# A streaming-encoder layer: an empty tile on the right stack, earlier queries, another bank for the gate scale

## The chip, the cores and the metric

The kernel runs on one core of one Trainium2 chip. The metric is the device time of one execution in microseconds (us), lower is better. Three timed runs of the kernel before gave 1702.1, 1703.69 and 1704.55 us; the median is 1703.69 us. The trace comes from one further, profiled execution.

## The reference, cut to what matters

One layer of a hybrid encoder on 1024 prompt tokens and 64 sample tokens, width 1024. Everything is f32.

```python
z = rmsnorm(x) @ w_in            # split: qa ka va (heads A) | qi ki wi (indexer) | qb kb vb (heads B) | ga gb (gates)
# A: isc[t,s] = sum_h wi[t,h] * relu(qi[t,h] . ki[s]); keep the top 256 keys (48 for samples); attention over them
# B: attention over the own 64-token chunk and the 8 chunks before, with a bias by relative distance
m = sigmoid(ga) * (oa @ w_o_a) + sigmoid(gb) * (ob @ w_o_b)
x = x + m @ w_out
y = x + square(relu(rmsnorm(x) @ w_up)) @ w_down
```

## The kernel before, in words

Tokens are worked on in nine blocks: 0 to 7 are the prompt (128 tokens each), block 8 holds the 64 samples. Each f32 product is made of three matmuls on high and low halves (`three`, L152), or two where one side is stacked (`two`, L161). The normalised input lies in SBUF turned, as `xnT` with high and low parts. A scheduler that works from an estimate of every instruction's time fixes the order of each engine's queue when the program is built: instructions that stand earlier in the program go first, and later ones fill in where an engine would be idle. `tc.issue_after(ins)` holds what its block issues on the engine of `ins` behind `ins`.

The stages that matter here, in order:

- **Indexer** (L392 to L472). `x` arrives in five pieces of 256 tokens (the last has 64). `cut_piece` splits a piece into `xnT`: eight copies on ACT (L267), eight subtractions on DVE (L268). `stage_keys(i)` multiplies block i with the 264 key columns, `stage_norms(i)` normalises and rotates the key (its last step is a GpSimd copy, L333), `stage_queries(i)` multiplies with the 320 query columns into a PSUM bank with the tag `acc` (two of them). `stage_scores(i)` first turns the key on TensorE into a bank `pt` (two of them; `index_keys`, L230: turn, ACT copy `kih`, DVE subtraction `kil`), then turns the queries, then makes the scores in banks `s` (four of them). Before, the order is: keys 0 to 5, scores 0 to 2, queries 4 and 5, piece 3, scores 3, keys 6 and 7, piece 4, scores 4, keys 8, queries 6 to 8.
- **Head projections** (`project_heads`, L512) and, beside them on DVE and ACT, the search for the top-k threshold (`choose`, L605). The results go through banks `acc` (2) and `wide` (4, which take the place of `s`, L598). `rows_to_dram` (L482) turns them in a bank `pt`.
- **Early gates** (L734 to L755): the first four rows of gate products, each three chunks of 24 matmuls in banks `wide` and `acc`. Each sum is multiplied on DVE with `spread` (L686), a tile that holds every token's scale on all partitions. `spread` is made by three sets of transposes (L731), in banks `pt`, each with an ACT copy (L733). The weights of these gates lie in the pool `pj`. `mask_out` (L661) then reads the scores in the pool `works` and writes the masks.
- **Attention** (L774 to L902): heads 0 to 7 of kind B, then 8 of kind A. `load_head` (L689) brings a head's `qT`, `kh`, `kl`, values and, for B, the bias (`turned`). Head 0 goes into a pool on the left and is loaded early; head 1 goes into `at`, on the right. `probs` (L781) records the first matmul of every score chunk in `marks`, 13 in a head. The eight middle rows of gates (L914) are fillers: 192 groups of three matmuls, of which group number i is held behind mark number i times 208/188 (`next_mark`, L908). Their weights come through `columns_of` (L762), which has its tiles in the pool `ring`: three `raw`, five `hi`, five `lo`.

SBUF pools are two stacks, `left` and `right`. On the right lie, from the outside: `fw` (8224 bytes a partition by its tiles: rope, five gains, two fold tiles, four rope temporaries), `works` (17824: the per-token scales and the scores), and on top of these first `ixw`, later `pj`, and `tk`. At L757 `tk`, `pj`, `works` and `fw` are closed; then `ring` is opened in their place (13 tiles of 2048 bytes: 26624) and `at` on top of it. `fw` and `works` end at byte 26048, where `pj` begins.

Of the kernel before, what the change touches and what calls it, by code (L numbers as in the profile page):

```python
# [10 lines left out]
F32 = mybir.dt.float32  # L11
# [7 lines left out]
P = 128  # L19
D = 1024  # L20
KB = D // P
TP = 1024
TS = 64
T = TP + TS
NT = TP // P
H = 8
HD = 64
# [17 lines left out]
def kernel(  # L45
# [8 lines left out]
    nc = tc.nc  # L54
# [26 lines left out]
    def bank(tag, n=512):  # L81
        pool, bufs = banks[tag]
        return pool.tile([P, n], F32, tag=tag, name=tag, bufs=bufs)
# [5 lines left out]
    def open_pool(name, side="left", **reuse):  # L89
        st = ExitStack()  # L90
        p = st.enter_context(tc.tile_pool(name=name, bufs=1, side=side, **reuse))
        pools[name] = st
        return p

    def close_pool(name):
        pools.pop(name).close()
# [4 lines left out]
    def acc():  # L101
        return bank("acc")

    def ptile():
        return bank("pt")
# [17 lines left out]
    def copy(out, in_):  # L123
        return nc.scalar.activation(out, in_, AF.Copy)  # L124

    last = {}
# [53 lines left out]
    xnT = xn_pool.tile([P, KB, 2, T], F32R, name="xnT")  # L180
# [13 lines left out]
    def project(i, ps, w, n):  # L194
        if i < NT:
            tok = slice(i * P, (i + 1) * P)
            last["projected"] = three(ps[:, :n], [((xnT[:, k, 0, tok], xnT[:, k, 1, tok]), w[k]) for k in range(KB)])
            return ps, P
        two(ps[:, :n], [(xsT[:, k, :], *w[k]) for k in range(KB)])
        hb = fw.tile([TS, 512], F32, tag="foldb", name="foldb", bufs=1)  # L200
        z = fw.tile([TS, 512], F32, tag="fold", name="fold", bufs=1)
        copy(hb[:, :n], ps[TS:P, :n])
        nc.vector.tensor_add(z[:, :n], ps[:TS, :n], hb[:, :n])
        return z, TS
# [59 lines left out]
    def split_piece(i, raws, k):  # L264
        c0, n = PIECES[i]
        hi, lo, raw = xnT[:, k, 0, c0:c0 + n], xnT[:, k, 1, c0:c0 + n], raws[k // 4][:, k % 4]
        last["piece"] = nc.scalar.activation(hi, raw, AF.Copy, scale=g_mix[:, k:k + 1])  # L267
        nc.vector.scalar_tensor_tensor(lo, raw, g_mix[:, k:k + 1], hi, op0=ALU.mult, op1=ALU.subtract)  # L268
# [35 lines left out]
    def stage_keys(i, ps=None):  # L304
        rows = P if i < NT else TS
        z1 = state.pop(i, None) or project(i, acc(), parts["keys"], 584 - SPLIT)[0]
        kd = ix.tile([P, 2, HD], F32, tag="kd", name="kd", bufs=6)
        ss = ix.tile([P, 8], F32, tag="ss", name="ss", bufs=6)
        jk = ix.tile([P, HD], F32, tag="jk", name="jk", bufs=1)
        nc.scalar.activation(jk[:rows], z1[:rows, 192:256], AF.Square, accum_out=ss[:rows, 0:1])  # L310
        nc.vector.tensor_copy(kd[:rows, 1, :], z1[:rows, 192:256])
        state[i] = (kd, ss)
        if i < 2:
            return
        qd = ix.tile([P, H, 2, HD], F32, tag="qd", name="qd", bufs=4)
        copy(qd[:rows, 5:8, 0, :], z1[:rows, :192].rearrange("p (h d) -> p h d", d=HD))
        aw = ix.tile([P, H], F32, tag="aw", name="aw", bufs=6)
        sg = ix.tile([P, H], F32, tag="sg", name="sg", bufs=6)
        nc.scalar.activation(aw[:rows], z1[:rows, 256:264], AF.Abs)
        nc.vector.tensor_scalar(sg[:rows], z1[:rows, 256:264], 0.0, 2.0, op0=ALU.is_ge, op1=ALU.mult)  # L320
        nc.gpsimd.tensor_scalar(sg[:rows], sg[:rows], -1.0, 1.0, op0=ALU.add, op1=ALU.mult)
        state[i] = (kd, ss, qd, aw, sg)
# [13 lines left out]
            nc.vector.tensor_scalar(aw[:rows], aw[:rows], scale, scale, op0=ALU.mult, op1=ALU.mult)  # L336
        state[i] = (kd, *rest)

    def stage_queries(i):
        if i < 2:  # L340
            return
        rows = P if i < NT else TS
        qd = state[i][-3]
        z0, _ = project(i, acc(), parts["queries"], SPLIT)
        copy(qd[:rows, 0:5, 0, :], z0[:rows, :320].rearrange("p (h d) -> p h d", d=HD))
        apply_rope(qd[:rows, :, 0, :], i, rows, H)
        nc.gpsimd.tensor_copy(qd[:rows, :, 1, :], qd[:rows, :, 0, :])

    def stage_scores(i, between={}):

        rows = P if i < NT else TS
        kd = state[i][0]
        if i == NT:
            cd = ix.tile([P, 2, HD], F32, tag="kd", name="cd", bufs=6)
            for a in range(2):
                nc.sync.dma_start(cd[:, a, :], cache_ki)
            index_keys(cd, P, TP)
            index_keys(kd, rows, TP + P)
        else:
            index_keys(kd, rows, i * P)  # L360
        if i < 2:
            return
        kd, qd, aw, sg = state.pop(i)
        qiT = ix.tile([P, H, P], F32R, tag="qiT", name="qiT", bufs=2)
        for j in range(2):
            ps = ptile()
            for q in range(4):
                nc.tensor.transpose(ps[:, q * rows:(q + 1) * rows],
                                    qd[:rows, 4 * j + q].rearrange("p a d -> p (a d)"), ident[:rows, :rows])
            v = ps[:, :4 * rows].rearrange("p (q r) -> p q r", q=4)  # L370
            dst = qiT[:, 4 * j:4 * j + 4, :rows]
            copy(dst, v)
            nc.vector.tensor_sub(dst[HD:P], v[HD:P], dst[HD:P])
        k0, n, wk = (0, P * (i + 1), work[i]) if i < NT else (TP, 192, work_s)
        for h in range(H):
            for c in range(0, n, 512):
                w = min(512, n - c)
                ps = bank("s")
                two(ps[:rows, :w], [(qiT[:, h, :rows], kih[:, k0 + c:k0 + c + w], kil[:, k0 + c:k0 + c + w])])
                r = ps  # L380
                nc.scalar.activation(r[:rows, :w], ps[:rows, :w], AF.Relu, scale=aw[:rows, h:h + 1])
                if h == 0:
                    nc.vector.tensor_scalar(wk[:rows, c:c + w], r[:rows, :w], sg[:rows, 0:1], None, op0=ALU.mult)
                else:
                    state["last"] = nc.vector.scalar_tensor_tensor(wk[:rows, c:c + w], r[:rows, :w], sg[:rows, h:h + 1],  # L385
                                                                   wk[:rows, c:c + w], op0=ALU.mult, op1=ALU.add)
            if h in between:
                next(between[h])
        if i < NT:
            nc.gpsimd.memset(wk[:TS, n - HD:n], HIDDEN)  # L390
# [21 lines left out]
        return raws  # L412

    def cut_piece(i, raws):
        for k in range(KB):
            split_piece(i, raws, k)

    for i in range(2):
        xts[i] = load_x(i)
# [12 lines left out]
    def norms(i):  # L432
        stage_norms(i)
        if i + 2 <= NT:
            xts[i + 2] = load_x(i + 2)
# [4 lines left out]
    cut_piece(2, x2)  # L440
    stage_keys(4)
    stage_keys(5)
    with tc.issue_after(last["projected"].ins):
        norms(2)
        norms(3)
        x4 = take_piece(4)
        for nm, g in (("qa", qnorm_a), ("ka", knorm_a), ("kb", knorm_b)):
            load(gains[nm], bcast(g, HD))
        for half in (slice(0, HD), slice(HD, P)):
            load(gain_qb[half], bass.AP(tensor=qnorm_b.tensor, offset=qnorm_b.offset, ap=[[1, HD], [1, 1]]))  # L450
        nc.gpsimd.tensor_scalar(gain_qb, gain_qb, HD ** -0.5, 1.0, op0=ALU.mult, op1=ALU.mult)
        for i in range(3):
            stage_scores(i)
    stage_queries(4)
    stage_queries(5)
    cut_piece(3, x3)
    with tc.issue_after(last["projected"].ins):
        norms(4)
        norms(5)
        stage_scores(3)  # L460
    stage_keys(6)
    stage_keys(7)
    cut_piece(4, x4)
    nc.vector.tensor_copy(xsT.rearrange("p k (a r) -> p k a r", a=2), xnT[:, :, :, TP:T])
    with tc.issue_after(last["projected"].ins):
        norms(6)
        stage_scores(4)
    stage_keys(8)
    for i in (7, 8):
        norms(i)  # L470
    for i in (6, 7, 8):
        stage_queries(i)  # L472
    close_pool("ixw")
    pj = open_pool("pj", "right")
    turn = iter([0] * FIRST + [0, 1, 1] * 200)

# [248 lines left out]
    first_head = load_head(*todo[0], kv)  # L725
    spread = xn_pool.tile([P, T], F32, tag="by_token", name="spread", bufs=1)
    for j in range(0, NT + 1, 4):
        ps, c0 = ptile(), 0
        for i in range(j, min(j + 4, NT + 1)):
            rows = P if i < NT else TS  # L730
            nc.tensor.transpose(ps[:, c0:c0 + rows], row_scale[:rows, i:i + 1].to_broadcast([rows, P]), ident[:rows, :rows])  # L731
            c0 += rows
        copy(spread[:, j * P:j * P + c0], ps[:, :c0])  # L733
    for g in range(0, EARLY, 4):  # L734
# [19 lines left out]
        with tc.issue_after(lows.ins):  # L754
            for j in range(6):  # L755
                mask_out(j)
    for nm in ("tk", "pj", "works", "fw"):  # L757
        close_pool(nm)

    ring = open_pool("ring", "right")  # L760
# [727 lines left out]
```

## Time and profile before

| what | value |
|---|---|
| timed runs, median (lowest to highest) | 1703.69 us (1702.1 to 1704.55) |
| profiled execution, its own time | 1701.1 us |
| its span in the trace | 1699.3 us |
| TensorE (PE) busy | 1678.4 us, 99% |
| VectorE (DVE), ScalarE (ACT), GpSimd (POOL) busy | 1169.3, 934.4, 393.1 us |
| mean granted TensorE clock | 0.996 |

Times in the trace are counted from the start of the span. Busy time of PE counts a matmul from its start to the end of its pipeline; what is not busy is time in which PE had no matmul in flight. [...] In a timeline row, the number in square brackets is the idle time of the engine ahead of the row and what ended it. SPq is the queue from which most DMAs are issued.

### The profile page before, as it was taken

The page shows a single profiled execution, that of the slowest core. Times are in us where ns is not written, and L with a number is a line of the kernel's source. Part 1 is how long each engine was busy: PE and PEld are TensorE (multiplying, and loading weights), DVE is VectorE, ACT ScalarE, POOL GpSimd, SP SyncE. Part 2 cuts the span into 40 slices and gives each one's busy share as a digit, 9 for nine tenths or more (in the row PEclk, how much of TensorE's full clock was granted, in tenths as well). Part 3 has the DMA queues.
Part 4 walks back from the last instruction along what each step waited for, and adds up shares of the span by engine and source line. Part 5 has one row for each costly group of instructions (what it writes and reads, how often), then busy time and mean ns, then how long its engine had stood idle before and what let it go on. Part 6 is the DMA issues. An engine that isn't in the chain of part 4 may idle for free.

```text
span 1699.3 us, 30465 instructions
## 1 busy us (share of the span) xinstructions
PE 1678.4 (99%) x10501; PEld 1543.6 (91%) x10501; DVE 1169.3 (69%) x2748; ACT 934.4 (55%) x1876; POOL 393.1 (23%) x524
## 2 busy tenths in 40 slices
PE   9999999999889999999999999999999999999999
PEld 8987888889889999999999999999999988888887
DVE  7855898879757788874454347666687649656794
ACT  8765688784256777774443347544454346343431
POOL 4434313506243343432343440000000000000000
PEclk9999999999989999999999999999999999999999
DMA  8135366663388877645544459555566599765652
GB/s 277 37 118 155 112 170 169 185 218 94 109 196 194 205 177 174 162 113 162 167 146 145 174 168 311 172 186 182 178 209 196 196 293 300 231 205 174 199 188 90
DMA packets 281195, 303.11 MB, mean 178 GB/s; under 512 B 40209, under 2 KB 202513, under 8 KB 281041
## 3 DMA queue, kind: packets, MB, share of 16 engines
q1 hardware_dynamic: 251920, 265.63, 54.0%
q10 hardware_dynamic: 29120, 35.53, 6.0%
q8 instruction: 83, 1.36, 0.3%
q14 instruction: 72, 0.58, 0.1%
HBM read 207.98 MB, written 93.08 MB: 177 GB/s over the span
## 4 chain that ended last, share of the span: by engine, by line
PE 70%; DMA 5%; DVE 3%; ACT 2%; issue 1%; POOL 1%; SPq 0%; ACTq 0%; DVEq 0%
PE x L156 6%; PE x L157 6%; PE x L158 6%; PE acc L156 6%; PE acc L158 6%; PE acc L157 6%; PE pt L814 3%; PE pg L156 2%; PE pe L156 2%; PE pg L158 2%; PE pe L158 2%; PE pe L157 2%; PE pg L157 2%; PE po L830 2%; PE s L164 2%; PE po L829 2%
## 5 line engine op out<-in xcount | busy, mean ns | idle before, releaser
L124 ACT ACTIVATE hi<-hw 128x1024 fp32r<-128x1024 f32 (+1 forms) x108 | 99.9, 932 | 159.2 <-PE x L158 56.3
L157 PE MATMUL x<-lo,hi 128*128 128x512 f32 (+1 forms) x440 | 169.5, 385 | 0.0
L158 PE MATMUL x<-hi,lo 128*128 128x512 f32 (+1 forms) x440 | 169.1, 385 | 0.0
L156 PE MATMUL x<-hi 128*128 128x512 f32 (+1 forms) x440 | 165.1, 385 | 0.0
L148 DVE TENSOR_TENSOR lo<-hw,hi 128x1024 fp32r<-128x1024 f32 (+1 forms) x108 | 113.8, 1061 | 47.9 <-ACT hi L124 46.5
L150 POOL TENSOR_TENSOR lo<-raw,hi 128x512 fp32r<-128x512 f32 x74 | 98.4, 1339 | 130.1 <-ACT hi L124 115.6
L124 ACT ACTIVATE hi<-raw 128x512 fp32r<-128x512 f32 x104 | 64.3, 626 | 96.3 <-PE acc L157 20.8
L622 ACT ACTIVATE nth<-work,cand 128x768 bf16<-128x768 f32 (+2 forms) x93 | 96.6, 1039 | 13.5 <-DVE cand L640 9.5
L826 DVE TENSOR_TENSOR pl<-pt,ph 128x512 fp32r<-128x512 f32 (+2 forms) x152 | 90.9, 615 | 16.7 <-ACT ph L124 16.3
L157 PEld LDWEIGHTS x<-lo,hi 128*128 128x128 f32 x440 | 82.7, 188 | 16.6
L156 PEld LDWEIGHTS x<-hi 128*128 128x128 f32 x440 | 82.7, 188 | 16.6
L158 PEld LDWEIGHTS x<-hi,lo 128*128 128x128 f32 x440 | 82.7, 188 | 16.5
L156 PE MATMUL acc<-xnT,hi 128*128 128x384 f32 (+1 forms) x288 | 97.2, 337 | 0.0
L157 PE MATMUL acc<-xnT,hi 128*128 128x384 f32 (+1 forms) x288 | 95.1, 330 | 0.0
L158 PE MATMUL acc<-xnT,lo 128*128 128x384 f32 (+1 forms) x288 | 94.9, 330 | 0.0
L157 PE MATMUL wide<-wlo,xnT 128*128 128x512 f32 x240 | 94.2, 394 | 0.0
L158 PE MATMUL wide<-whi,xnT 128*128 128x512 f32 x240 | 93.7, 391 | 0.0
L156 PE MATMUL wide<-whi,xnT 128*128 128x512 f32 x240 | 92.2, 394 | 1.3 <-DVE work_s L385 1.3
L124 ACT ACTIVATE ph<-pt 128x512 fp32r<-128x512 f32 (+3 forms) x168 | 80.1, 514 | 23.3 <-PE pt L814 18.6
L801 POOL TENSOR_SCALAR mw<-mw,sm 128x640 f32<-128x640 f32 (+1 forms) x64 | 56.7, 885 | 127.6 <-DVE sm L800 123.4
L164 PE MATMUL s<-kh,qT 128*128 128x384 f32 (+4 forms) x208 | 77.1, 372 | 3.5 <-DMA kh<-kT_b 1.9
L830 PE MATMUL po<-pl,vhl 128*128 128x256 f32 (+1 forms) x304 | 79.5, 293 | 0.4 <-DVE pl L826 0.3
(693 smaller groups left out, 5731.9 us busy)
## 6 DMA issues: line engine op xcount, KB each, us to landing
hw<-h SPq DMA_DIRECT2D x108, 256.0 KB, 3.1
hw<-in_w_down_dram SPq DMA_DIRECT2D x108, 256.0 KB, 3.7
wraw<-in_w_in_dram SPq DMA_DIRECT2D x56, 256.0 KB, 2.8
h<-h ACTq DMA_DIRECT2D x32, 272.0 KB, 2.2
raw<-in_w_out_dram SPq DMA_DIRECT2D x32, 256.0 KB, 3.0
raw<-in_w_up_dram SPq DMA_DIRECT2D x32, 256.0 KB, 3.4
out_dram<-t SPq DMA_DIRECT2D x24, 256.0 KB, 2.8
g_dram<-gate SPq DMA_DIRECT2D x32, 192.0 KB, 2.4
```

Of the source, the lines that this page charges most:

```text
L124: return nc.scalar.activation(out, in_, AF.Copy)
L148: last["lo"] = nc.vector.tensor_sub(lo, raw, hi)
L150: nc.gpsimd.tensor_sub(lo, raw, hi)
L156: nc.tensor.matmul(out, sh, mh, start=(opens and i == 0), stop=False, skip_group_check=resumes)
L157: nc.tensor.matmul(out, sh, ml, start=False, stop=False, skip_group_check=resumes)
L158: last = nc.tensor.matmul(out, sl, mh, start=False, stop=(closes and i == n - 1), skip_group_check=resumes)
L164: first = nc.tensor.matmul(out, s, mh, start=(i == 0), stop=False)
L622: nc.scalar.activation(sign[:, :w.shape[1]], w, AF.Sign, bias=against, scale=-1.0, accum_out=col(cnt, j))
L801: nc.gpsimd.tensor_scalar(m[:rows, :n], m[:rows, :n], sm[:rows, 6:7], 1.0, op0=ALU.mult, op1=ALU.mult)
L814: nc.tensor.transpose(ps[:krows, oo:oo + qrows], m[:qrows, kc:kc + krows], ident[:qrows, :qrows])
L826: nc.vector.tensor_sub(pl[:kr, a:b], ps[:kr, a:b], ph[:kr, a:b])
L830: nc.tensor.matmul(dst, vhl[:krows, vt, :], pl[:krows, oo:oo + width], start=False, stop=(idx == n - 1))
```

## The change

There are three parts. First, `stage_queries` takes a bank tag; queries 4 and 5 move ahead of the block that holds scores 0 to 2 and use banks `s`, so that the key turns (transposes) of scores 0 to 2 are held behind the last matmul of queries 5; `norms` 2 and 3 stand ahead of these queries, and are no longer in the block; the ACT copies of pieces 3 and 4 are held behind the ACT copy of the last queries staged; scores 3 lose their hold; queries 6 move ahead of piece 4 and keys 8. Second, an empty pool `gap` of 192 f32 (768 bytes a partition) is opened on the right stack after `ixw` is closed and before `pj` is opened; it is closed with `pj`. Third, the three sets of transposes for `spread` use a bank `wide` in place of a bank `pt`. No arithmetic is added or left out.

```diff
-    def stage_queries(i):
-        if i < 2:
-            return
+    def stage_queries(i, tag="acc"):
...
-        z0, _ = project(i, acc(), parts["queries"], SPLIT)
-        copy(qd[:rows, 0:5, 0, :], z0[:rows, :320].rearrange("p (h d) -> p h d", d=HD))
+        z0, _ = project(i, bank(tag), parts["queries"], SPLIT)
+        last["queries"] = copy(qd[:rows, 0:5, 0, :], z0[:rows, :320].rearrange("p (h d) -> p h d", d=HD))
...
     def cut_piece(i, raws):
-        for k in range(KB):
-            split_piece(i, raws, k)
+        with tc.issue_after(last["queries"].ins) if i > 2 else ExitStack():
+            for k in range(KB):
+                split_piece(i, raws, k)
...
     stage_keys(5)
+    norms(2)
+    norms(3)
+    stage_queries(4, "s")
+    stage_queries(5, "s")
     with tc.issue_after(last["projected"].ins):
-        norms(2)
-        norms(3)
         x4 = take_piece(4)
...
         for i in range(3):
             stage_scores(i)
-    stage_queries(4)
-    stage_queries(5)
     cut_piece(3, x3)
-    with tc.issue_after(last["projected"].ins):
-        norms(4)
-        norms(5)
-        stage_scores(3)
+    norms(4)
+    norms(5)
+    stage_scores(3)
     stage_keys(6)
     stage_keys(7)
-    cut_piece(4, x4)
-    nc.vector.tensor_copy(xsT.rearrange("p k (a r) -> p k a r", a=2), xnT[:, :, :, TP:T])
     with tc.issue_after(last["projected"].ins):
         norms(6)
         stage_scores(4)
+    stage_queries(6)
+    cut_piece(4, x4)
+    nc.vector.tensor_copy(xsT.rearrange("p k (a r) -> p k a r", a=2), xnT[:, :, :, TP:T])
     stage_keys(8)
     for i in (7, 8):
         norms(i)
-    for i in (6, 7, 8):
+    for i in (7, 8):
         stage_queries(i)
     close_pool("ixw")
+    open_pool("gap", "right").tile([P, 192], F32, name="shift_heads")
     pj = open_pool("pj", "right")
...
     for j in range(0, NT + 1, 4):
-        ps, c0 = ptile(), 0
+        ps, c0 = bank("wide"), 0
...
-    for nm in ("tk", "pj", "works", "fw"):
+    for nm in ("tk", "pj", "gap", "works", "fw"):
         close_pool(nm)
```

## The prediction

> **What bounds the kernel now.** I read the page first, then the waits of PE, then PE's own timeline at each of its pauses, then the windows with the granted clock.
>
> ```profile
> span 1699.3 us, 30465 instructions
> PE 1678.4 (99%) x10501; PEld 1543.6 (91%) x10501; DVE 1169.3 (69%) x2748; ACT 934.4 (55%) x1876; POOL 393.1 (23%) x524
> PE 70%; DMA 5%; DVE 3%; ACT 2%; issue 1%; POOL 1%; SPq 0%; ACTq 0%; DVEq 0%
> ```
>
> PE is the bound, and the change takes no matmul away. All that can be won is PE's idle time, 1699.3 - 1678.4 = 20.9 us, and time in which PE ran at a lower clock. PE's timeline shows where most of the idle time lies (in brackets: idle us, releaser):
>
> ```profile
> 35.01 0.33 PE L232 MATMUL pt<-ident,kd 128*128 128x128 f32 x1 [2.39 <-POOL kd L333]
> 35.62 0.39 PE L156 MATMUL acc<-wqh,xnT 128*128 128x320 f32 x1 [0.28 <-DVE by_row L284]
> 430.36 0.65 PE L731 MATMUL pt<-ident,by_row 128*128 128x128 f32 x4 [1.31 <-DVE pair L491]
> 434.30 0.85 PE L731 MATMUL pt<-ident,by_row 128*128 128x128 f32 x5 [1.38 <-DVE pair L491]
> 435.69 0.44 PE L156 MATMUL wide<-xnT,whi 128*128 128x384 f32 x1 [0.55 <-DVE gate L686]
> 469.08 0.38 PE L829 MATMUL po<-ph,vhl 128*128 128x256 f32 x1 [0.42 <-ACT ph L124]
> 471.38 0.44 PE L164 MATMUL s<-kh,qT 128*128 128x128 f32 x1 [1.92 <-DMA kh<-kT_b]
> 472.94 0.45 PE L165 MATMUL s<-kl,qT 128*128 128x128 f32 x1 [1.12 <-DMA kl<-kT_b]
> 477.93 0.69 PE L164 MATMUL s<-kh,qT 128*128 128x384 f32 x1 [0.89 <-DVE sm L794]
> 493.01 0.30 PE L843 MATMUL po<-ph,vhl 128*128 128x64 f32 x1 [2.09 <-ACT ph L124]
> ```
>
> There are three places: the second key turn at 35, the spread transposes at 430, and the start of attention at 460 to 495. Each part of the change touches one. The third is the dearest, since the clock falls there too. Windows cut at the falls (PE busy, then the other engines; PEclk; DMA share; GB/s):
>
> ```profile
> 448.00:460.00 12.00, 12.00 (x75) 11.93 (x74) 4.71 (x8) 1.87 (x3) 1.05 (x1) 1.00 0.29 86
> 460.00:470.90 10.90, 8.27 (x46) 5.79 (x44) 9.19 (x38) 8.51 (x23) 4.94 (x10) 1.00 0.87 181
> 470.90:481.60 10.70, 8.21 (x35) 7.59 (x35) 3.04 (x13) 2.96 (x9) 3.23 (x5) 0.52 1.14 226
> 481.60:494.80 13.20, 11.08 (x78) 10.39 (x77) 6.65 (x23) 8.30 (x22) 7.19 (x9) 1.00 0.87 187
> 494.80:498.60 3.80, 3.80 (x13) 3.73 (x13) 3.10 (x12) 2.57 (x6) 1.35 (x4) 0.55 0.95 271
> 498.60:1699.30 1200.70, 1196.67 (x8011) 1132.53 (x8009) 790.24 (x1641) 604.43 (x1174) 204.05 (x235) 1.00 0.63 189
> ```
>
> From 460 to 498.6 PE is idle for 2.63 + 2.49 + 2.12 = 7.24 us. At clocks of 0.52 and 0.55, 8.21 us of busy time holds 4.27 us of full-speed work and 3.80 us holds 2.09, so the clock costs 3.94 + 1.71 = 5.65 us. Together 12.9 us are lost here. From 498.6 to the end PE is idle for 4.0 us in 1200.7 at full clock.
>
> **Part A, queries 4 and 5 ahead of the key turns.** Before, PE is done with keys 5 and key turn 0 by 35.01 - 2.39 = 32.6 and meets key turn 1, whose key is not ready. After, it has 48 query matmuls to do first.
>
> ```profile
> 35.62:39.21 3.59, 3.59 (x24) 3.59 (x25) 3.56 (x21) 3.20 (x16) 1.81 (x8) 1.00 0.79 258
> 28.92 1.72 ACT L267 ACTIVATE xnT<-xc,g_mix 128x256 fp32r<-128x256 f32 x4
> 31.09 1.71 ACT L267 ACTIVATE xnT<-xc,g_mix 128x256 fp32r<-128x256 f32 x4
> 33.41 0.47 DVE L268 SCALAR_TENSOR_TENSOR xnT<-xc,g_mix,xnT 128x256 fp32r<-128x256 f32 x1
> 36.43 0.29 ACT L124 ACTIVATE kih<-pt 128x128 fp32r<-128x128 f32 x1
> 37.33 0.28 DVE L234 TENSOR_TENSOR kil<-pt,kih 128x128 fp32r<-128x128 f32 x1
> 40.06 0.42 ACT L124 ACTIVATE qd<-acc 128x320 f32<-128x320 f32 x1
> ```
>
> The two queries last 2 x 3.59 = 7.2 us, from about 32.4 to 39.6. The key of the 2.39 us pause was there at 35.0, so that wait goes. The 0.28 us wait belongs to queries 4 in an `acc` bank that keys had just left; in an `s` bank it goes too. Removed: 2.67 us. But queries 5 were the cover of what follows, and that cover is gone. Key turns 0 to 2 and the turned queries now come one after the other through two `pt` banks, each held for a copy (0.29) and a subtraction (0.28). And piece 3, which ACT cut from 28.9 to 32.8, is now held behind the copy of queries 5: its first part is ready at the earliest 0.42 + 0.43 + 0.47 = 1.3 us after queries 5 (0.43 is 1.72/4). From then on each part of 0.43 us feeds blocks 6 and 7, six matmuls; by the window above these are 0.15 us each or 0.9 us (somewhat less, for 264 columns), so PE is fed. New pause: 0 if the turns fill it, 1.3 by the first part, at worst the whole piece, 0.42 + 3.43 + 0.47 = 4.3 us, if nothing of it is used on the way. I take 1.0, near the first part's row, as some turns do fit in. ACT and DVE, free of piece 3 from 28.9 on, do norms 2 and 3 sooner. The moved norms issue only their own steps and x loads ahead of the same SP queue; the loads of piece 4 and of the gains come later in program order, and piece 4 is needed only by keys 8. **A: -1.7 us (bounds -2.7 and +1.6).**
>
> **Part B, spread in a wide bank.** Before, its transposes wait for `pt` banks, held by turned queries of kind A until DVE, deep in the masks, gets to their subtraction (L491). PE has filled all six gate banks by then, as no gate sum leaves without spread. The scales themselves were ready long before.
>
> ```profile
> 431.05 0.60 ACT L124 ACTIVATE spread<-pt 128x512 f32<-128x512 f32 x1 [2.75 <-PE pt L731]
> 415.92 0.68 DVE L535 TENSOR_TENSOR t<-wide,rs 128x512 f32<-128x512 f32 x1
> 418.26 0.68 DVE L535 TENSOR_TENSOR t<-wide,rs 128x512 f32<-128x512 f32 x1
> ```
>
> DVE frees two of the four wide banks only at 416.6 and 418.9. The other two serve the first gate chunks from 404 on, so spread has a bank at about 404, or at the latest when those two come free, 12 us ahead of 430. A set holds its bank for 0.65 us of transposes and 0.60 us of copy. Then gate sums leave as they end, and the waits of 1.31 + 1.38 + 0.55 = 3.24 us go. If a wide bank comes no sooner than the `pt` bank did, nothing goes. The first set of three may cost one bank hold, so I take less than the whole. **B: -2.8 us (bounds -3.3 and 0).**
>
> **Part C, the empty tile.** It computes nothing. It moves `pj` by 768 bytes. Without it `ring` (26624 bytes) reaches 576 bytes beyond `works` (which ends at 26048), into `pj`, whose weights the last early gate reads. With it `ring` ends inside the empty tile. The trace shows what `ring` waited for (SP's queue, its waits, the tiles):
>
> ```profile
> 453.17 4.48 SPq L687 DMA_DIRECT2D g_dram<-gate  x2
> 460.30 0.48 SPq L695 DMA_DIRECT2D qT<-qT_b  x1
> 468.33 4.67 SPq L767 DMA_DIRECT2D raw<-in_w_in_dram  x3
> SPq L695 <- PE acc L158: 2.5, 1, 2.5
> L668 DVE TENSOR_SCALAR seen<-work,thr x6: 412/712/1684, 412.1 to 445.0; 128x384 bf16<-128x384 f32 x1, 128x512 bf16<-128x512 f32 x1, 128x640 bf16<-128x640 f32 x1, 128x768 bf16<-128x768 f32 x1
> L124 ACT ACTIVATE hi<-raw x5: 613/630/632, 478.0 to 492.2; 128x512 fp32r<-128x512 f32 x5
> L150 POOL TENSOR_TENSOR lo<-raw,hi x5: 1266/1283/1295, 479.5 to 493.6; 128x512 fp32r<-128x512 f32 x5
> ACT hi L124: 11.6, 4
> 477.57 0.29 DVE L794 CUSTOM_DVE_ANT_0 m<-s,turned 128x128 f32<-128x128 f32 x1 [7.04 <-DMA turned<-in_rel_rows_dram]
> ```
>
> SP stood idle before 460.3, although the last reader of `works` was done at about 445.8 and raws need only free bytes. It issued the loads of head 1 (in `at`, released by the last gate matmul) and then, at 468.3, the first raw. So I infer that `ring` waits for the whole of `pj`, not for the bytes that it shares. After, raws can go at about 446, into DMA engines that are busy for 0.29 of the time. Five splits of 0.63 (ACT) and 1.28 us (POOL, 6.4 in all) end well before 460. So the filler groups are ready when their marks are.
>
> From 460.2 the loads of head 1 keep their time: its bias comes 17.4 us later (DVE's 7.04 us wait for it ends at 477.57), and DVE can't start head 1 before. What has PE to do in these 17.4 us? Before, up to 477.6 it did 8.27 us of head 0, then, in 6.7 us with 0.48 + 1.12 = 1.6 idle, (6.7 - 1.6) x 0.52 = 2.7 us. After, it has besides the groups of head 0's 13 marks and head 1's first two, 15 x 3 x 0.16 = 7.2 us (12.00/75 = 0.16 a matmul). That makes 18.2 us of work, and fills the stretch. With the pauses filled the clock should stay up, and ACT no longer stands behind `hi` copies that wait for raws (11.6 us in four waits, ahead of the 2.09 us pause too). Of the 12.9 us I leave 2.9: about 2 for the start of the softmax chain and fillers that the scheduler puts later than their marks, 0.9 for the rest. If only half of the 15 groups come ahead (3.6 us lost) and the clock falls as before (5.65), 3.7 us remain. **C: -10.0 us (bounds -12.9 and -3.7; 0 if the ring is not what holds the raws).**
>
> In the rows above the clock fell to a half after pauses of 0.42 and 1.92 us within 3 us, none longer. [...]
>
> **The sum.** -1.7 - 2.8 - 10.0 = -14.5 us. The profiled execution took 1701.1 us (span 1699.3 and 1.8 around it), which gives 1686.6. It lay 2.6 us under the median, 1703.69, to which the same gain is applied: 1689.2 us. As PE is full from 498.6 on, a gain made by then is kept.
>
> **Rivals.** *The clock falls anyway*: the start of attention has many short turns and small matmuls, and the low clock may come from these. For it: it fell after short pauses. Against: in the window at 481.6 PE worked at full clock on the same kinds. The gain lacks 5.65 us: 8.9, or 1694.8 us. *The ring is not what holds the raws*: scheduler order or another pool does, and they still follow head 1's loads. For it: the waits show SP held by PE for head 1's load, no such row for the raws themselves. Then A and B remain: 4.5, or 1699.2 us. *Slower*: ACT's hold on piece 3. PE starves for the whole piece, 4.3 us at 40, and the clock falls there for as long as at 471, where it cost about 4 us. For it: DVE was 3.56 of 3.59 us busy there, so nothing catches up. Against: parts are used one by one. A becomes -2.7 + 4.3 + 4 = +5.6; this decides the sign once B and C bring less than that, so only where the ring gives nothing: 5.6 - 2.8 = +2.8, or 1706.5 us.
>
> **How the numbers follow.** Forecast 0.62 (its own range 1685 to 1693), clock 0.14, ring 0.14, slower 0.05, other small changes 0.05. About 0.2%, 3.4 us, is what a measurement of this kernel can tell from no change, so faster means under 1700.3. Faster: 0.62 + 0.14 + two thirds of the ring rival, about 0.85. Within: the rest of that and most of the small changes, 0.09. Slower: 0.06. The range runs from A and B at their best with C at -12.9 (rounded to 1684.5) to 1698.5, which takes in the clock rival and leaves out half of the ring rival and the slower cases.
>
> **What would show it.** Right: raws (L767) issued at 440 to 455, `hi` copies done before head 1's loads, gate matmuls in `acc` from the first marks on; no fall of the clock between 460 and 500; no wait of L731 for L491; at 35 no pause, and one of about 1 us near 40. Wrong: raws still behind head 1's loads; the clock at a half in spite of filled pauses; a pause of several us at 40 behind L267.

## The result, and the profile after

The changed kernel took 1692.3 us (median of six runs, 1691.06 to 1693.06), the kernel before 1704.01 us (1701.13 to 1704.76) beside it. The ratio is 0.9934, with a 95% interval of 0.9921 to 0.9947: 11.7 us faster by the medians, where the forecast was 14.5. The total lies in the range, but its parts do not add up as forecast: tried alone, the first part cost time.

The page after, its lines 1 and 4:

```profile
span 1691.2 us, 30465 instructions
PE 1672.3 (99%) x10501; PEld 1539.8 (91%) x10501; DVE 1166.2 (69%) x2748; ACT 935.7 (55%) x1876; POOL 389.4 (23%) x524
PE 74%; DMA 2%; DVE 2%; issue 1%; ACT 1%; POOL 1%; SPq 0%; DVEq 0%; ACTq 0%
```

The span is 8.1 us shorter and not 11.7, as the profiled execution of after was the slowest of its six (1693.06 us), and that of before, with 1701.1, was 2.9 under its median. PE is still the bound; DMA went from 5% to 2% of the chain. The windows across the start of attention, cut at the fall of the clock (length, PE busy, PE weight loads, DVE, ACT, POOL, granted TensorE clock as a share of full speed, DMA share, GB/s):

```profile
460.80:465.20 4.40, 1.83 (x13) 1.56 (x12) 1.34 (x6) 1.52 (x5) 3.85 (x6) 1.00 0.71 173
465.20:468.60 3.40, 3.40 (x14) 3.30 (x13) 1.26 (x6) 0.76 (x3) 0.85 (x2) 0.50 0.95 237
468.60:480.00 11.40, 11.40 (x83) 11.25 (x82) 9.09 (x33) 8.55 (x22) 4.44 (x6) 1.00 1.08 222
480.00:499.40 19.40, 18.30 (x134) 16.96 (x132) 13.77 (x52) 12.36 (x33) 6.48 (x11) 1.00 0.85 208
```

Idle time here is 2.57 + 1.10 = 3.67 us and the lower clock costs, by its granted share, 3.40 x 0.5 = 1.7, together 5.4 where 12.9 were lost before. The clock still fell, once. The stretch from the last early gate to the last `po` holds the same matmuls in both kernels; first before, then after:

```profile
460.20:777.65 317.45, 309.80 (x2224) 299.90 (x2223) 240.62 (x831) 223.51 (x555) 126.50 (x182) 0.98 0.72 171
```

```profile
461.10:768.89 307.79, 303.74 (x2224) 296.57 (x2224) 239.28 (x831) 222.41 (x551) 123.31 (x180) 0.99 0.73 174
```

It is 9.7 us shorter. SP's queue shows what moved:

```profile
452.29 1.48 SPq L767 DMA_DIRECT2D raw<-in_w_in_dram  x3
457.63 2.07 SPq L767 DMA_DIRECT2D raw<-in_w_in_dram  x2
459.75 0.50 SPq L687 DMA_DIRECT2D g_dram<-gate  x1
461.81 1.59 SPq L767 DMA_DIRECT2D raw<-in_w_in_dram  x2
463.50 0.44 SPq L687 DMA_DIRECT2D g_dram<-gate  x1
464.55 0.37 SPq L767 DMA_DIRECT2D raw<-in_w_in_dram  x1
465.01 0.54 SPq L695 DMA_DIRECT2D qT<-qT_b  x1
```

The raws leave at 452, 16 us sooner than before and ahead of head 1's loads, but head 1's first load now leaves at 465.0, where it left at 460.3. With the raws early, the first weights of a filler group (`acc<-xnT,hi`) are loaded into PE at 464.1 us, at 479.3 before. PE's timeline at its larger pauses:

```profile
40.53 0.39 PE L156 MATMUL acc<-wkh,xnT 128*128 128x264 f32 x1 [0.70 <-ACT xnT L267]
50.87 0.66 PE L366 MATMUL pt<-ident,qd 128*128 128x128 f32 x4 [1.70 <-DVE qiT L371]
59.51 0.66 PE L366 MATMUL pt<-ident,qd 128*128 128x128 f32 x4 [1.58 <-DVE qiT L371]
60.75 0.39 PE L164 MATMUL acc<-wkh,xsT 128*128 128x264 f32 x1 [0.58 <-DVE ms L131]
226.51 0.46 PE L485 MATMUL pt<-ident,t 64*128 64x64 f32 x4 [0.86 <-POOL t L538]
332.85 0.66 PE L485 MATMUL pt<-ident,t 128*128 128x128 f32 x4 [1.02 <-POOL t L214]
463.68 0.33 PE L164 MATMUL s<-kh,qT 128*128 128x128 f32 x1 [2.57 <-DVE gate L686]
```

The 2.39 us at 35 and the waits of L731 at 430 are gone. In their place stand 4.56 us between 40 and 61, two pauses in the head projections, and a new kind of wait at 463.

### The profile page after: what moved, and what is told of

Read it like the earlier page. It is cut to its first block, busy times and chain, and to the rows that moved or that the text cites. A ratio compares the mean times of both kernels' runs of the same rounds, so it can differ in the third digit from the quotient of the medians.

```text
span 1691.2 us, 30465 instructions
## 1 busy us (share of the span) xinstructions
PE 1672.3 (99%) x10501; PEld 1539.8 (91%) x10501; DVE 1166.2 (69%) x2748; ACT 935.7 (55%) x1876; POOL 389.4 (23%) x524
## 4 chain that ended last, share of the span: by engine, by line
PE 74%; DMA 2%; DVE 2%; issue 1%; ACT 1%; POOL 1%; SPq 0%; DVEq 0%; ACTq 0%
PE acc L156 6%; PE acc L158 6%; PE acc L157 6%; PE x L156 6%; PE x L157 6%; PE x L158 6%; PE pt L814 3%; PE po L830 2%; PE pg L156 2%; PE pe L156 2%; PE pg L158 2%; PE pe L158 2%; PE pe L157 2%; PE pg L157 2%; PE s L164 2%; PE s L165 2%
## 5 line engine op out<-in xcount | busy, mean ns | idle before, releaser
L158 PE MATMUL x<-hi,lo 128*128 128x512 f32 (+1 forms) x440 | 169.1, 385 | 0.0
L826 DVE TENSOR_TENSOR pl<-pt,ph 128x512 fp32r<-128x512 f32 (+2 forms) x152 | 91.6, 615 | 14.5 <-ACT ph L124 14.0
L158 PEld LDWEIGHTS x<-hi,lo 128*128 128x128 f32 x440 | 82.6, 188 | 16.5
L158 PE MATMUL acc<-xnT,lo 128*128 128x384 f32 (+1 forms) x288 | 94.8, 329 | 0.0
L158 PE MATMUL wide<-whi,xnT 128*128 128x512 f32 x240 | 93.8, 391 | 0.0
```

The lines of the kernel that those rows point to most:

```text
L158: last = nc.tensor.matmul(out, sl, mh, start=False, stop=(closes and i == n - 1), skip_group_check=resumes)
L826: nc.vector.tensor_sub(pl[:kr, a:b], ps[:kr, a:b], ph[:kr, a:b])
```

## The experiments

Three marks from PE's timeline serve most of them: the first matmul of the head projections into a `wide` bank, the last early gate matmul, and the last `po`. "Idle" is PE's idle time between the first two, over the same 1440 matmuls. Clock times in the last column start at the fall and say how long the clock stayed at a half. Gains in us below are worked out from the ratio.

| kernel | first wide | idle to the last gate | last gate to last po | span | clock at a half |
|---|---|---|---|---|---|
| before | 163.06 | 3.83 | 317.74 | 1699.3 | 471.0 (10.2), 494.9 (3.4) |
| after | 165.69 | 2.34 | 308.09 | 1691.2 | 465.2 (3.4) |
| c_only | 165.79 | 4.27 | 304.33 | 1688.9 | 34.9 (6.8) |
| b_only | 164.28 | 0.47 | 317.35 | 1696.9 | 34.6 (3.4), 468.1 (6.8), 488.6 (6.8) |
| a_only | 165.70 | 4.98 | 316.42 | 1704.5 | 439.5 (3.4), 477.0 (10.2) |
| no_a | 165.34 | 0.23 | 306.88 | 1687.1 | 35.6 (3.4), 462.2 (3.4) |
| a_no_hold | 161.67 | 3.86 | 316.26 | 1695.6 | 470.3 (6.8), 490.8 (3.4) |
| a_q_only | 165.15 | 0.73 | 316.57 | 1696.2 | 461.5, 475.2, 492.3 (3.4 each) |
| no_hold | 161.28 | 1.60 | 307.61 | 1685.5 | 460.3 (3.4) |
| no_hold_actq | 163.59 | 0.33 | 306.61 | 1684.1 | 48.5 (3.4) |
| gap_128 | 164.50 | 3.29 | 315.95 | 1698.8 | 436.7 (3.4), 474.3 (6.8), 494.8 (3.4) |
| gap_144 | 166.25 | 3.26 | 303.04 | 1693.1 | 35.4 (3.4) |
| actq | 166.42 | 0.30 | 307.66 | 1688.4 | 34.5 (6.8) |
| best | 166.74 | 2.25 | 304.05 | 1689.0 | 39.9, 166.2 (3.4 each) |

### The parts one by one

**The empty tile alone (c_only)**: the kernel before with these two lines.

```diff
+    open_pool("gap", "right").tile([P, 192], F32, name="shift_heads")
     pj = open_pool("pj", "right")
...
-    for nm in ("tk", "pj", "works", "fw"):
+    for nm in ("tk", "pj", "gap", "works", "fw"):
```

> The kernel before with the empty tile alone (768 bytes). Ring theory: the first raws are issued some 10 us ahead of the last early gate matmul instead of 8 us behind it, gate fillers run from the first marks on, the half clock is gone or shorter, and 8 to 10 us are won from the end of the early gates on. What it costs in the head projections, if the two pauses of about 1 us each at 225 and 333 in the kernel after belong to the moved pj, is about 2.5 us, so 1694 to 1697 us. Rival (the tile only shifts addresses, the gain comes from the spread or the queries): under 2 us won, raws at the same place, 1702 to 1704 us.

Measured: 1689.1 us against 1702.4, ratio 0.9928 (0.9916 to 0.994), so 12.3 us, more than was expected. The stretch of attention in its windows, and its start:

```profile
463.80:767.76 303.96, 302.10 (x2223) 294.91 (x2222) 239.61 (x831) 222.08 (x550) 120.29 (x177) 1.00 0.72 173
463.43:502.00 38.57, 37.09 (x262) 35.39 (x261) 28.10 (x106) 24.77 (x65) 15.47 (x26) 1.00 0.92 213
```

13.5 us less than before's 317.45, 1.48 us idle in its first 38.6, and the clock stays at 1.00. The raws lead in SP's queue:

```profile
449.37 0.38 SPq L768 DMA_DIRECT2D raw<-in_w_in_dram  x1
464.53 0.48 SPq L696 DMA_DIRECT2D qT<-qT_b  x1
```

This one part alone brings as much as the whole change.

**The wide bank alone (b_only)**:

```diff
-        ps, c0 = ptile(), 0
+        ps, c0 = bank("wide"), 0
```

> The kernel before with the wide bank for the spread alone. By the trace of after, where the early gates last 4.3 us less: -3 to -4.5 us, 1699.5 to 1701 us. Rival (the gates were quicker there only because the first part or the tile moved DVE's work): 1703 to 1704 us, with the waits of L731 replaced by waits for wide banks.

Measured: 1698.68 us, ratio 0.998 (0.9971 to 0.9989), 3.4 us. The waits of L731 are gone, idle in this stretch falls from 3.83 to 0.47.

**The indexer's part alone (a_only)**: the changed kernel with the other two edits taken back.

> The kernel before with the changes to queries, norms, pieces and scores alone. The prediction had -1.7 us. By the trace of after, whose first wide matmul starts 2.6 us later than before: slower by 2 to 3 us, 1706 to 1707 us, with pauses of about 1.7 and 1.6 us at 50 and 59 behind turned queries. Rival (the loss at the first wide matmul is made up later, or was a matter of that execution): within 1 us of before. If the pauses at 225 and 333 belong to this part, another 2.5 us are lost.

Measured: 1705.14 us, ratio 1.0018 (1.001 to 1.0027): slower by 3.1 us. The head projections reach their first wide bank 2.6 us later than before.

**Without it (no_a)**: the empty tile and the wide bank together.

> The empty tile and the wide bank, without the first part. If the first part loses 2.6 us and the others win what after shows, 1689 to 1690 us, faster than after by 2 to 3 us. Rival (the parts hang together, and the early raws or the gates need the queries' order): as after or slower, 1692 to 1694 us.

Measured: 1690.91 us, ratio 0.9934 (0.9922 to 0.9946), just that of the changed kernel, and no better than the empty tile alone (0.9928). So the two do not add up. The wide bank frees 4.0 us of idle time ahead of the last gate (4.27 to 0.23), and attention takes 2.6 us more (304.33 to 306.88). PE's timeline of this kernel holds the new wait too, followed by a fall of the clock:

```profile
460.89 0.39 PE L164 MATMUL s<-kh,qT 128*128 128x256 f32 x1 [2.64 <-DVE gate L687]
```

### How long the empty tile must be

The empty tile alone, with 128 or 144 f32 in place of 192: 512 or 576 bytes, the shared bytes being 576.

> The kernel before with an empty tile of 128 f32, 512 bytes, 64 bytes too short for the ring to clear pj by the tiles' sizes (576 needed). Ring theory: the first raw stays behind the loads of head 1, some 8 us after the last early gate matmul, and the clock falls there as before; from the last early gate matmul to the 200th value matmul (po) it takes about 112 us as before. Rival (any shift of pj does it, by the order or by the addresses): raws ahead of the last gate matmul and about 99 us, as with 768 bytes.

> The same with 144 f32, 576 bytes, which is just enough. Ring theory: as with 768 bytes, the first raw some 10 to 14 us ahead of the last early gate matmul, about 99 us from there to the 200th value matmul. Rival: no difference to 512 bytes.

Measured, one run each: 1700.68 us with 512 bytes, 1695.06 with 576. SP's queue, with 512 bytes:

```profile
462.45 0.48 SPq L696 DMA_DIRECT2D qT<-qT_b  x1
470.43 4.41 SPq L768 DMA_DIRECT2D raw<-in_w_in_dram  x3
```

and with 576:

```profile
453.39 0.38 SPq L768 DMA_DIRECT2D raw<-in_w_in_dram  x1
468.14 0.47 SPq L696 DMA_DIRECT2D qT<-qT_b  x1
```

With 64 shared bytes left, the raws stay behind head 1's loads, and attention takes 315.95 us from the last gate to the last `po`; with none left they lead, and it takes 303.04 (to the 200th `po`: 109.3 and 95.6, before 111.1). The first filler weights are loaded at 480.4 and at 468.6. The whole time differs by 5.6 us only, as the last early gate came 5.4 us later with 576 bytes (467.46 and 462.06). So it is the overlap, not a shift of addresses as such, that held the raws. By which way it held them is not shown: where there is an overlap, no raw has a wait for PE of its own on record. The raws stand in SP's queue behind head 1's first load, which waited 2.50 us for PE's last early gate (L158), and the order of that queue is the scheduler's. Without an overlap the first raw waits for DVE's last read of the scores (L668 in the kernel before).

### What the indexer's part loses

**Its holds taken out (a_no_hold)**: a_only, with the copies of pieces 3 and 4 not held.

```diff
 def cut_piece(i, raws):
-        with tc.issue_after(last["queries"].ins) if i > 2 else ExitStack():
-            for k in range(KB):
-                split_piece(i, raws, k)
+        for k in range(KB):
+            split_piece(i, raws, k)
```

> The first part alone, without ACT's holds on pieces 3 and 4 (the order of the program stays as in the part). Theory: the holds leave DVE and ACT idle for about 7 us each between 20 and 40 us and put this work beside the query turns after 40; both pauses of 1.6 us (at 51 and 60, PE waiting for DVE's subtraction of turned queries) come from that. Without the holds these pauses are under 1 us together and the first wide matmul starts 2 to 3 us sooner than in the part with them (165.7), at 163 to 164 us. Rival (the pauses come from the place of queries 4 and 5, whose matmuls no longer cover the turns): pauses of over 2 us in all at 40 to 62, and the first wide matmul at 165 to 166 us.

Measured: 1698.65 us, ratio 0.9989 (0.9977 to 1.0001); that interval lies below a_only's, but takes in no change against the kernel before. The first wide bank comes at 161.67, 1.4 us before the old order's and 4.0 before a_only's. The windows from 39.7 to 62, first of a_only, then without the holds:

```profile
39.70:62.00 22.30, 17.80 (x125) 16.29 (x124) 19.83 (x81) 19.13 (x58) 8.95 (x30) 1.00 0.25 68
```

```profile
39.70:62.00 22.30, 21.53 (x154) 20.64 (x155) 20.77 (x85) 17.58 (x51) 9.76 (x39) 1.00 0.11 28
```

4.50 us of idle become 0.77. What the holds do is in ACT's timeline of the changed kernel:

```profile
36.12 0.44 ACT L124 ACTIVATE qd<-s 128x320 f32<-128x320 f32 x1 [1.28 <-PE s L158]
39.64 0.44 ACT L124 ACTIVATE qd<-s 128x320 f32<-128x320 f32 x1 [3.08 <-PE s L158]
...
56.44 1.77 ACT L267 ACTIVATE xnT<-xc,g_mix 128x64 fp32r<-128x64 f32 x7
58.11 0.58 ACT L124 ACTIVATE qiT<-pt 128x512 fp32r<-128x512 f32 x1
```

ACT waits 1.28 and 3.08 us for PE while piece 3 could be cut, and the copies of pieces 3 and 4 then fall among the query turns: seven of piece 4's stand ahead of the `qiT` copy at 58.11, whose subtraction on DVE ends the pause at 59.51. The hold also reaches further than the pieces: the squares of the next norms (L281) are held behind the last piece cut (L280), so the two that came at 32.7 and 34.2 us before come at 43.5 and 44.5, and the `xt` loads behind them leave at 44.7 and not at 35.5.

**The queries alone (a_q_only)**: the kernel before, with `stage_queries(4, "s")` and `stage_queries(5, "s")` behind `stage_keys(5)`, and nothing else moved.

> The kernel before with queries 4 and 5 in score banks ahead of scores 0 to 2, and nothing else of the first part: norms 2 and 3, pieces, scores 3 and 4 and queries 6 stay. Theory: the wait for key 1 at 35 us is covered, the pieces are cut early as before, and the first wide matmul starts 1 to 2.7 us sooner than before in an execution whose clock did not fall at 35 (163.06), at 160.5 to 162 us. Rival (the cover of the key turns is gone, as the prediction priced it with 1.0 us and at most 4.3): a pause of over 1.5 us at 40 to 45 and the first wide matmul at 163 us or later. The two pauses of about 1 us in the head projections may come in either case, as the order there is fixed anew.

Measured: 1694.73 us, ratio 0.9969 (0.996 to 0.9979), 5.3 us by the ratio. But not where it was looked for. PE's pauses in the indexer are 0.78, 0.70 and 2.40 us, and the first wide bank comes 2.1 us later than before. What the profile shows of the gain (its execution, 1698.0, was the slowest of ten) is in the early gates: idle falls from 3.83 to 0.73. With this order the spread has one wait for `pair`, of 0.6 us, where it had two of 1.31 and 1.38, though its banks are still `pt`. So what a wide bank is worth depends on the schedule ahead of it.

**The changed kernel without its holds (no_hold)**:

> The changed kernel with one thing taken out: the copies of pieces 3 and 4 on ACT are not held behind the copy of queries. Theory (the holds are what made the first part lose: with them the heads of the first part alone began at 76.5 us, without them at 72.1): PE's pauses in the indexer between 38 and 62 fall from 4.6 us (0.70 + 1.70 + 1.58 + 0.58) to about 1, the head projections begin at 72 to 73 (76.0 in the changed kernel), their stretch from the first wide bank to the last gate is 292 to 293 (295.1), the wait for the first gates' store at 463 stays at about 2.6; median 1687 to 1689, ratio to the kernel before 0.991 to 0.992. Rival (the new order of queries and norms costs by itself, and the holds' loss was an accident of one execution): heads at 75 to 76, the two pauses at L366 stay, 1691 to 1693, ratio 0.993 to 0.995.

Measured: 1688.2 us (1685.03 to 1692.45) against 1701.66, ratio 0.9925 (0.9906 to 0.9944). The first wide bank comes at 161.28 (165.69 with the holds), and one pause of 0.76 us is left between 39.7 and 62. The median points the way expected; the interval overlaps that of the changed kernel.

### The wait at the start of attention

**Raws from ACT's queue (actq)**: no_a, and the first eight raws go through another queue.

```diff
+    early_raws = [nc.scalar] * 8
...
-        nc.sync.dma_start(raw, src.rearrange("(k p) c -> p k c", p=P))
+        (early_raws.pop() if early_raws else nc.sync).dma_start(raw, src.rearrange("(k p) c -> p k c", p=P))
```

> The empty tile and the wide bank, with the first eight raws issued from ACT's queue and not from SP's. Theory: with the wide bank the early gates end some 5 us sooner, but the masks, and so the raws, do not; SP then stands at raws that wait for GpSimd's splits, a gate store waits behind them, DVE for the gate tile and PE for DVE (2.6 us), and the clock falls for 3.4 us. With the raws out of SP's queue this pause and this fall go: 3 to 4.5 us under the kernel with both parts, 1686.5 to 1688 us. Rival (the pause comes from the splits or the masks themselves, not from the queue): the same 2.6 us pause, no gain, 1690 to 1691 us; or ACT stands at a raw's wait instead and PE waits for the softmax.

Measured: 1688.76 us, ratio 0.9918 (0.9905 to 0.993), which overlaps no_a's and is not the 1686.5 to 1688 expected. PE's timeline from 456 to 470:

```profile
460.31 0.39 PE L164 MATMUL s<-kh,qT 128*128 128x256 f32 x1 [0.86 <-DVE gate L687]
465.21 0.33 PE L817 MATMUL pt<-ident,m 128*128 128x128 f32 x1 [1.73 <-POOL m L804]
465.73 0.44 PE L817 MATMUL pt<-ident,m 128*128 128x128 f32 x2 [0.19 <-POOL m L804]
```

The wait for DVE's gate falls from 2.64 to 0.86 us, so SP's queue made 1.8 us of it. How, the changed kernel shows, in SP's waits (us in all, times, longest) and in DVE's timeline:

```profile
SPq L767 <- POOL lo L150: 5.2, 4, 1.7
```

```profile
463.14 0.49 DVE L686 TENSOR_TENSOR gate<-acc,spread 128x320 f32<-128x320 f32 x1 [4.06 <-DMA g_dram<-gate]
```

SP stands at raws that wait for POOL's `lo`; the store of a gate leaves behind them at 459.75, DVE waits for that store, and PE for DVE. DVE's wait for a store is 4.28 us in no_a and still 2.60 in actq. But a wait for POOL of 1.73 us comes up 5 us later, and attention takes as long as in no_a (307.66 and 306.88). The clock does not fall there any more.

**One query block ahead (best)**: actq with `stage_queries(4, "s")` ahead of scores 0 to 2, and `stage_queries(5)` left in its place.

> As the run before, and queries 4 alone, in a score bank, ahead of scores 0 to 2; queries 5, the pieces and the norms stay where they were before. Theory: 3.6 us of queries 4 cover the wait for key 1 (2.4 to 3.3 us, with the clock at a half behind it in some executions), and queries 5 stay as the cover of the key turns, so that nothing comes back: 2.5 to 4 us under the run without it, 1683 to 1686 us. Rival (the pause comes back at the key turns, as with the whole first part): no gain or a loss of up to 2 us.

Measured: 1691.34 us, ratio 0.9936 (0.9923 to 0.9949): not better. The first wide bank comes at 166.74, with two falls of the clock (39.9 and 166.2, 3.4 us each), and a pause of 1.55 us appears at 230. The pause at 35 was not covered but moved: queries 5, in an `acc` bank, now start at 39.0 after 2.72 us of waiting for DVE (L320), which had still to read keys out of that bank.

**Without holds, and raws from ACT's queue (no_hold_actq)**:

> As the run without the holds, and the first eight raw weight blocks of the gates are issued from ACT's queue in place of SP's. Theory (two separate losses, which add: holds, some 4 us by 72 us; SP's queue, 2.57 us at 463): heads at 72 to 73, no pause over 1.8 us at 460 to 470, last matmul at 1680 to 1682, median 1684 to 1687, ratio 0.989 to 0.991, faster than every kernel so far (the lowest median is 1688.8). Rival (what is won by 72 us is lost again later, as with queries 4 alone ahead, whose heads began early and whose median was 1691.3): pauses of over 0.5 us appear in the head projections at 225 or 332, median 1688 to 1691.

Measured: 1685.85 us (1684.51 to 1686.45) against 1701.66, ratio 0.9907 (0.9887 to 0.9927). It is the lowest median of all kernels, and its runs span less than no_hold's. Against the changed kernel's ratio (from 0.9921) the intervals overlap by a little, so that it beats the changed kernel is likely, not shown to 95%. Its first wide bank came 2.3 us later than no_hold's, at 163.59; the fall of the clock at 48.5 makes 1.7 of that.

## Why the prediction was right in sum, and where it was wrong

**C, the empty tile: right, in mechanism and size.** -10.0 was forecast. Alone it brought 12.3 us, inside the bounds and near the better one; in the changed kernel attention is 9.7 us shorter. That the overlap with `pj` holds the raws was an inference from one row; the tiles of 512 and 576 bytes show it. That `ring` waits for the whole of `pj`, and not for the tile that lies in the shared bytes, is not shown by them. Three things under this step failed. The raws left at 449.4 (c_only) and 452.3 us, not at about 446, and the five splits that were to end "well before 460" lasted on POOL from 456.1 to 464.5 in the changed kernel. Head 1's loads do not "keep their time": with raws that wait on SP ahead of them they left 4.7 us later. And "with the pauses filled the clock should stay up" held in c_only, where they were filled (1.48 us idle in 38.57, clock 1.00); in the changed kernel they were not, as a new pause of 2.57 us came in at 463. The prediction had raws move ahead of head 1's loads, and priced no wait of SP on the raws' own tiles.

**B, the wide bank: right alone, and a larger term than forecast** (-2.8; measured -3.4, both as idle time and in the runs). But the terms were simply added: with C, gates that end sooner bring no more, since the raws are not sooner (449.4 in c_only, 449.3 in no_a, whose last gate comes at 457.8 and not 463.4), and part of the time is waited for at 460 to 464. On top of C it measures nothing.

**A, the queries: wrong in sign.** Forecast -1.7 with a bound of +1.6; measured +3.1 us alone (+2.6 at the first wide bank). The failed step is "New pause ... I take 1.0, near the first part's row". In place of 1.0 stand 4.56 us. The pause at 40 was near the forecast, 0.70 us, so piece 3 does feed PE part by part. What was not followed is the hold past that point: two further pauses of 1.70 and 1.58 us, both at query turns. At the second, piece 4's cuts stand in front on ACT and DVE; at the first, the turn's copy (49.42) stood behind a square of `xt` that had waited for its load, one of those that left 9 us late. Both are gone without the holds. "ACT and DVE, free of piece 3 from 28.9 on, do norms 2 and 3 sooner" was the wrong picture as well: their squares come at 26.5 and 27.8 us, before at 26.2 and 27.5, and ACT stood waiting. Without the holds the same order brings 1.4 us at the first wide bank (1.8 in no_hold), near the -1.7 of the forecast; the runs (0.9989) do not tell it from no change. One gain was not counted: of seven traces in the old order five show a fall of the clock at the pause of 35, for 3.4 or 6.8 us, 1.7 or 3.4 us of work; the one profile shown had none. That may be why the loss in the runs (3.1) is smaller than between the two spans (5.2). Beside the other two parts the loss does not show at all: the changed kernel and no_a have the same ratio, and no_a's profile has the fall at 35.6.

**The sum.** A came out 4.8 us worse than forecast and C 2.3 better, and B, whose 2.8 were added, brought nothing beside C. That the total still missed by 3 us only is in part luck.

**The rivals.** "The clock falls anyway" fell: c_only has the same short turns and no fall after 41.7. "The ring is not what holds the raws" fell with the 512 and 576 bytes. The slower rival had the right culprit, ACT's hold, and about the right loss for it, 4.0 us at the first wide bank by a_only against a_no_hold (4.3 was its price), but not its place: no long starving at 40. Its condition, that the ring gives nothing, did not come.

**What stays open.** In c_only the idle time and the clock at the start of attention account for 12.9 - 1.5 = 11.4 us, yet the stretch is 13.5 us shorter. PE's busy time for the same matmuls is 7.7 us less, of which 5.65 are the clock's. What makes the other 2 us was not tested. Nor were the pauses in the head projections followed to their cause (at 332: 1.02 us after, 1.18 in a_only, none there in no_hold).

## What to carry to other kernels

A pool that reuses the space of closed pools can be tied to the last use of one that it hardly touches; here 64 shared bytes a partition were enough. Compare the byte ends of old and new pools, and pay a few hundred bytes to part them. When loads become early, look at what is queued behind them, and on whom they wait themselves; a gain upstream of that point can end up in it. A hold that gives an engine a better order can leave it idle where it had work, and later holds hang on it: try the order without the hold first.

## What was not expected of the hardware

Between 20 and 1600 us the 14 traces of this case show 25 stretches at a granted clock of 0.50; each lasts 3.4, 6.8 or 10.2 us. In the 3.4 us right ahead of them PE was idle for 1.25 to 3.23 us (before: 2.00 ahead of 471.0 and 1.52 ahead of 494.9; after: 1.92 ahead of 465.2), in no case for all of the time. As much idle time also passed with no fall behind it: in before 2.39 us in the 3.4 us up to 35.01, in after 1.70 us in the 3.4 us up to 50.87. The two ranges overlap, so these traces give no limit. The pause at 35 alone, whose falls begin between 34.5 and 35.6 us, shows the same: 2.39 us (before) and 2.72 us (gap_128) brought no fall, while 2.64 to 3.28 us in c_only, b_only, no_a, gap_144 and actq brought 3.4 to 6.8 us at a half. What parts them is not shown. Where the prediction says "none longer", the fall at 494.9 stands behind the longer pause of 2.09 us, of which about 1.5 lie in the 3.4 us right ahead of it. Nor does one long pause stand ahead of every fall. The windows of no_hold_actq around 48.5:

```profile
44.40:48.50 4.10, 2.47 (x18) 2.02 (x17) 3.05 (x21) 3.53 (x12) 1.14 (x7) 1.00 0.04 10
48.50:51.90 3.40, 3.40 (x15) 3.31 (x14) 3.25 (x10) 2.86 (x6) 0.72 (x4) 0.50 0.11 24
```

The fall came behind two pauses of 0.87 and 0.77 us, with no longer one in these 4.10 us. By the granted share it cost 3.40 x 0.5 = 1.7 us of work.
